# Strassen pairs of w_up: relu and squares behind the next pair's first copy, weight splits beside earlier work

## The chip, the cores and the metric

One NeuronCore of a Trainium2 chip runs the whole program in one launch. The metric is device time in microseconds, the median of several executions. Below, PE is TensorE, ACT ScalarE, DVE VectorE, POOL GpSimd and SP SyncE; POOL and SP only issue DMAs at the places spoken of here.

## The reference

Two transformer layers (`DEPTH = 2`) and then one further layer of another kind, over 1024 tokens of width 1024 in float32. What the change touches is the feed-forward part of the first two layers, of width 4096:

```python
for i in range(DEPTH):
    ...
    hn = rmsnorm(h, norm2[i])
    h = h + jnp.square(jax.nn.relu(hn @ w_up[i])) @ w_down[i]
    ...
```

## The kernel before

Every float32 operand of a matmul is split into a high part, which is float32r, and a low part, the remainder; a product is three matmuls (high by high, high by low, low by high) that add up in one bank of PSUM. A matmul has a stationary 128x128 weight and 512 moving columns. A split of a 128x1024 tile is a copy on ACT (`whi` or `hidh`) and a subtraction on DVE (`wlo` or `hidl`).

`w_up` has 32 output tiles of 128 rows, called units. Units 0 to 7 and 30, 31 are plain (`up`: 8 tiles of the contraction by 3 matmuls by 2 halves of 512 tokens, 48 in all). Units 8 to 29 are computed in pairs by Strassen's scheme, with 7 products instead of 8: 11 pairs in each layer. A product (`prod`, line 1210) is 4 tiles of the contraction by 3 matmuls, 12 in all; a pair is 84. The products come in this order: 1 (A11) into bank P, 2 (S2) into Q, 3 (A12) again into P, 4 (S3) again into Q, 5 (S1) into R, 6 (A22) again into Q, 7 (S4) again into R. Between them ACT and DVE take the banks out: `t1` is ACT's copy of P after product 1 (line 1236), which product 3 must wait for since it adds into the same bank; `u2` and `u3` are DVE's sums of Q and t1; `c1` and `c2` are the two result tiles, to which relu and square are applied on ACT before POOL stores them to DRAM (`keep`, line 1122, tensor `hidd`).

The weights of a pair come as two tiles (`wst`, three buffers, loaded by SP in the order of a plan). `seven` (line 1071) is a generator that splits them, and forms the sums that the scheme wants, into 7 tiles `wsp` out of a ring of 8 buffers, which plain units' `whi` and `wlo` share. Its steps are: A11 and A12 together, A22, four sums on DVE, S2, S3 and S1 together, S4. During a pair the steps of the next pair's weights are called by hand between the products: the first after product 4, two after 5, one after 6, the rest after 7. The weights of the first pair are split in one go behind unit 7.

All engines run their instructions in the order in which the program issues them. Background work is called by `tick`: `spawn` registers a generator that is advanced once for so many microseconds of matmuls, and `advance` splits the weights of plain units up to two ahead, as long as no more than four are held.

After the pairs, units 30 and 31 are plain, and then `w_down` is done in 8 chunks of 4 hid tiles: `fetch` loads the 4 raw tiles of a chunk from `hidd` by POOL, `parts` splits them (`hidh`, `hidl`), and PE adds up products `pd`. The h tiles to which these are added are loaded by POOL behind the first fetch.

Of the kernel before, what the change touches and what calls it, by code (L numbers as in the profile page):

```python
# [2 lines left out]

# [13 lines left out]
AF = mybir.ActivationFunctionType  # L17
# [51 lines left out]
class K:  # L69
# [117 lines left out]
    RAW = ("old", "mg", "w_out2")  # L187

    def is_raw(self, key):
        return key[0] in self.RAW or key[0] == "w_up" and self.SEVEN[0] <= key[2] < self.SEVEN[1]  # L190

    def source(self, key):
        name = key[0]
# [918 lines left out]
    def mlp(self, i, nm, h):  # L1112
# [3 lines left out]
        nc = self.nc  # L1116
        nm.rest(h)
        xs = nm.xs
        box = {}
        lo_, hi_ = self.SEVEN  # L1120

        def keep(m, t):
            nc.gpsimd.dma_start(self.hidd[m], t)

        def up(m, turns=False):
            t = []

            def done(ps, cs):
                if not t:
                    t.append(self.st("hid"))  # L1130
                if "xs" in box:
                    nc.scalar.activation(t[0][:, cs], ps, AF.Relu)
                else:
                    nc.vector.scalar_tensor_tensor(t[0][:, cs], ps, 0.0, box["bc"][:, cs], OP.max, OP.mult)

            self.gemm(("w_up", i, m), xs, done, turns)
            nc.scalar.activation(t[0], t[0], AF.Square)
            keep(m, t[0])

# [21 lines left out]
        def sums():  # L1161
            for p in range(4):
# [13 lines left out]
                b = None  # L1176
                yield

        ta, tb = [], []
        ps = [self.pair("pu") for _ in range(2)]  # L1180
        self.duo([("w_up", i, m) for m in range(2)], xs, ps, cols)
# [4 lines left out]
        for m, pp in enumerate(ps):  # L1186
            t = self.st("hid")
# [4 lines left out]
        t = ps = None  # L1192
        up(3, True)
        xs = nm.xs = None
        box["go"] = True
        self.finish(box["apply"])
        xs = box["xs"] = box.pop("new")
        box["bc"] = None
        sm = self.spawn(sums(), 2.4)
        up(4, True)  # L1200
        for m in range(5, lo_):
            up(m)
            if m == lo_ - 2:
                self.finish(sm)
        A, B = self.HALVES
        view = lambda ts, cs: [(hi[:, cs], lo[:, cs]) for hi, lo in ts]
        x = {"B11": view(xs[0:4], A), "B21": view(xs[4:8], A), "B22": view(xs[4:8], B),
# [2 lines left out]
        def prod(ps, wn, xn, first=False, last=False):  # L1210
            mm = nc.tensor.matmul
            wh, wl = w[wn]
            for k, (xh, xl) in enumerate(x[xn]):
                c = slice(k * 128, (k + 1) * 128)
                mm(ps, wh[:, c], xh, start=first and k == 0, stop=False, skip_group_check=True)  # L1215
                mm(ps, wh[:, c], xl, start=False, stop=False, skip_group_check=True)
                mm(ps, wl[:, c], xh, start=False, stop=k == 3, skip_group_check=True)  # L1217
                if k % 2:
                    self.tick(1.36)
# [1 line left out]
        self.live, self.gone = self.SPLIT_BUFS, []  # L1221
        add = lambda o, p, q: nc.vector.tensor_tensor(o, p, q, OP.add)  # L1222
        pairs = list(range(lo_, hi_, 2))
        gen = self.seven(*[("w_up", i, lo_ + e) for e in range(2)])
        for w in gen:
            pass
        for m in pairs:
            ahead = iter(())
            nxt = None
            if m + 2 < hi_:  # L1230
                ahead = self.seven(*[("w_up", i, m + 2 + e) for e in range(2)])
            P, Q, R = (self.bank("p7") for _ in range(3))
            t1, u2, u3 = (self.k2("u7") for _ in range(3))
            c1, c2 = (self.st("hid") for _ in range(2))
            prod(P, "A11", "B11", True)
            nc.scalar.activation(t1, P, AF.Copy)  # L1236
            prod(Q, "S2", "T2", True)
            add(u2, Q, t1)
            prod(P, "A12", "B21")
            nc.scalar.activation(c1[:, A], P, AF.Relu)  # L1240
            prod(Q, "S3", "T3")
            add(u3, Q, t1)
            nxt = next(ahead, None)
            prod(R, "S1", "T1", True)
            add(c2[:, B], u3, R)
            next(ahead, None)
            next(ahead, None)
            prod(Q, "A22", "T4")
            add(c2[:, A], Q, t1)
            nc.scalar.activation(c2, c2, AF.Relu)  # L1250
            next(ahead, None)
            prod(R, "S4", "B22")
            add(c1[:, B], u2, R)
            nc.scalar.activation(c1[:, B], c1[:, B], AF.Relu)
            for _ in ahead:
                pass
            for n, t in enumerate((c1, c2)):
                nc.scalar.activation(t, t, AF.Square)
                keep(m + n, t)
            t = c1 = c2 = P = Q = R = t1 = u2 = u3 = None  # L1260
            w = nxt
        x = w = ta = tb = nxt = ahead = gen = None
        box.pop("apply")
        self.drop(self.SPLIT_BUFS)

        def fetch(c):
            r = [self.st("hid") for _ in range(4)]
            for q in range(4):
                nc.gpsimd.dma_start(r[q], self.hidd[4 * c + q])
            return r  # L1270

        raw = fetch(0)
        for k in range(8):
            h[k] = self.st("h")
            nc.gpsimd.dma_start(h[k], self.hd[k])
        hid = []

        def parts(n):
            for _ in range(n):
                hid.append(self.split(raw.pop(0), "hid"))  # L1280

        up(30)
        parts(2)
        up(31)
        xs = box["xs"] = None
        parts(2)
        nn = self.norm(self.g[:, i * 24 + 16:i * 24 + 24])
        for c in range(8):
            now, hid = hid, []
# [773 lines left out]
```

## Time and profile before

| what | value |
|---|---|
| median of 3 runs | 3298.48 us (3297.35 to 3300.71) |
| the profiled execution | 3301.77 us, span 3300.0 us |
| busy share of the span: PE, DVE, ACT, POOL | 96%, 59%, 39%, 9% |
| pairs of the first layer | about 513 to 745 us of the span |
| pairs of the second layer | about 1736 to 1969 us of the span |

The page says how long each engine was busy. Who waited for whom is a view of its own, with the total, the count and the longest wait. The order of time lists every instruction with its start, its duration and, in brackets, how long its engine was idle before it and what ended that. A matmul's duration overlaps with the next one's, so the distance of two starts tells the pace.

### The profile page before, as it was taken

How to read it: one execution, taken by the hardware profiler on the slowest of the kernel's cores; microseconds unless marked ns; L12 is line 12 of the kernel's file. 1: busy time of each engine (PE TensorE's matmuls, PEld its weight loads, DVE VectorE, ACT ScalarE, POOL GpSimd, SP SyncE). 2: the span in 40 equal slices, each digit the busy share in tenths (PEclk: the TensorE clock that was granted, in tenths of full speed). 3: DMA queues.
4: the chain of work that ended last, by engine and by line, in shares of the span. 5: the costliest groups of instructions: out<-in, count | busy, mean ns of one | idle time of the engine just before them, and what ended most of it. 6: DMA issues, size and time to landing. Idle time of an engine off the chain costs nothing. (4 is left out here: it accounts for less than half of the span.)

```text
span 3300.0 us, 39088 instructions
## 1 busy us (share of the span) xinstructions
PE 3176.3 (96%) x15332; PEld 2644.0 (80%) x15332; DVE 1961.0 (59%) x3044; ACT 1287.3 (39%) x2128; POOL 312.0 (9%) x479
## 2 busy tenths in 40 slices
PE   8999999999999999999999989999999999999998
PEld 7888787777888888888887777888888787788877
DVE  7666564443444556666564443444655888887465
ACT  4666343333111323666343332111333555554330
POOL 5122000001000002121000011000000000001100
PEclk9999999999999999999999999999999999999999
DMA  4112332335222113222422335222113333335561
GB/s 157 45 51 77 118 112 80 102 102 220 92 96 90 40 50 121 57 58 66 143 87 91 98 107 222 102 97 65 45 39 110 83 95 78 86 90 147 159 211 64
DMA packets 94681, 326.33 MB, mean 99 GB/s; under 512 B 13552, under 2 KB 13728, under 8 KB 94496
## 3 DMA queue, kind: packets, MB, share of 16 engines
q1 hardware_dynamic: 50256, 178.11, 17.0%
q0 software_dynamic: 42944, 141.25, 14.4%
q10 hardware_dynamic: 1296, 4.46, 0.3%
q8 instruction: 121, 1.98, 0.2%
q14 instruction: 64, 0.52, 0.1%
HBM read 244.93 MB, written 75.69 MB: 97 GB/s over the span
## 5 line engine op out<-in xcount | busy, mean ns | idle before, releaser
L311 ACT ACTIVATE whi<-wst 128x1024 fp32r<-128x1024 f32 x214 | 223.4, 1054 | 678.8 <-PE pd L261 498.7
L260 PE MATMUL pd<-hidh,whi 128*128 128x512 f32 x1024 | 400.4, 391 | 2.7 <-ACT hidh L323 2.7
L261 PE MATMUL pd<-hidl,whi 128*128 128x512 f32 x1024 | 400.7, 391 | 1.8 <-DVE hidl L324 1.8
L262 PE MATMUL pd<-hidh,wlo 128*128 128x512 f32 x1024 | 400.1, 391 | 0.0
L1307 DVE TENSOR_TENSOR h<-pd,h 128x512 f32<-128x512 f32 x256 | 175.6, 690 | 332.3 <-PE pd L262 332.3
L316 DVE TENSOR_TENSOR wlo<-wst,whi 128x1024 fp32r<-128x1024 f32 x172 | 207.8, 1223 | 100.7 <-ACT whi L311 100.1
L260 PE MATMUL w_in<-nh,whi 128*128 128x512 f32 x560 | 229.6, 410 | 4.9 <-DVE wl L1600 3.6
L260 PEld LDWEIGHTS pd<-hidh,whi 128*128 128x128 f32 x1024 | 193.0, 188 | 43.5 <-ACT hidh L323 3.6
L261 PEld LDWEIGHTS pd<-hidl,whi 128*128 128x128 f32 x1024 | 193.1, 189 | 43.1 <-DVE hidl L324 3.3
L262 PEld LDWEIGHTS pd<-hidh,wlo 128*128 128x128 f32 x1024 | 193.2, 189 | 40.1
L261 PE MATMUL w_in<-nl,whi 128*128 128x512 f32 x560 | 221.1, 395 | 0.0
L262 PE MATMUL w_in<-nh,wlo 128*128 128x512 f32 x560 | 221.0, 395 | 0.0
L518 PE MATMUL pa<-xh,whi 128*128 128x512 f32 x448 | 181.4, 405 | 0.0
L519 PE MATMUL pa<-xl,whi 128*128 128x512 f32 x448 | 177.0, 395 | 0.0
L520 PE MATMUL pa<-xh,wlo 128*128 128x512 f32 x448 | 177.0, 395 | 0.0
L1541 DVE SCALAR_TENSOR_TENSOR cv<-sg,n,cv 128x1023 f32<-128x1023 f32 (+14 forms) x120 | 151.4, 1262 | 0.6
L1215 PE MATMUL p<-nh,wsp 128*128 128x512 f32 x264 | 106.8, 405 | 34.5 <-ACT u L1236 29.1
L260 PEld LDWEIGHTS w_in<-nh,whi 128*128 128x128 f32 x560 | 106.8, 191 | 24.6 <-DVE wl L1600 4.0
L262 PEld LDWEIGHTS w_in<-nh,wlo 128*128 128x128 f32 x560 | 106.6, 190 | 23.6
L261 PEld LDWEIGHTS w_in<-nl,whi 128*128 128x128 f32 x560 | 107.1, 191 | 18.7 <-issue 0.5
L695 ACT ACTIVATE E<-E,stat 128x256 f32<-128x256 f32 (+1 forms) x192 | 87.7, 458 | 65.2 <-DVE stat L693 65.1
L1222 DVE TENSOR_TENSOR u<-p,u 128x512 f32<-128x512 f32 x44 | 30.4, 691 | 135.8 <-PE p L1217 114.5
(455 smaller groups left out, 7595.9 us busy)
## 6 DMA issues: line engine op xcount, KB each, us to landing
wst<-in_w_up_dram SPq DMA_DIRECT2D x64, 512.0 KB, 4.1
hidd<-hid POOLq DMA_DIRECT2D x64, 512.0 KB, 7.0
wst<-in_w_down_dram SPq DMA_DIRECT2D x64, 512.0 KB, 3.7
hid<-hidd POOLq DMA_DIRECT2D x64, 512.0 KB, 6.1
wst<-in_w_in_dram SPq DMA_DIRECT2D x40, 512.0 KB, 4.3
wst<-in_w_qkv_dram SPq DMA_DIRECT2D x36, 512.0 KB, 4.1
wlo<-in_w_in_dram POOLq DMA_DIRECT2D x35, 512.0 KB, 5.7
wst<-in_w_out_dram SPq DMA_DIRECT2D x24, 512.0 KB, 4.2
```

Source lines behind the costliest of these rows:

```text
L260: mm(ps, wh, xh[:, cs], start=k == 0, stop=False)
L261: mm(ps, wh, xl[:, cs], start=False, stop=False)
L262: mm(ps, wl, xh[:, cs], start=False, stop=k == n - 1)
L311: nc.scalar.activation(h, w, AF.Copy)
L316: nc.vector.tensor_tensor(l, w, h.bitcast(F32), OP.subtract)
L518: mm(out, wh, xh, start=k == 0, stop=False)
L519: mm(out, wh, xl, start=False, stop=False)
L520: mm(out, wl, xh, start=False, stop=k == 7)
L695: nc.scalar.activation(Eh, Eh, AF.Exp, scale=-1.0, bias=stat[:, j, h:h + 1], accum_out=stat[:, j, 4 + h:5 + h])
L1215: mm(ps, wh[:, c], xh, start=first and k == 0, stop=False, skip_group_check=True)
L1307: lambda ps, cs: nc.vector.tensor_tensor(h[m][:, cs], ps, h[m][:, cs], OP.add))
L1541: nc.vector.scalar_tensor_tensor(acc[:, d:1024], C[:, 0:1024 - d], cw[:, j, 30 - d:31 - d], acc[:, d:1024], OP.mult, OP.add)
```

## The change

What a pair does to its result at the end (relu of half of c1, two squares, two stores) becomes a function `post`, which is called in the next pair right behind the copy t1, and behind the last pair once more. The first pair's weights are split by a background generator during unit 7 (the first five steps of `seven`) and the rest behind unit 7. Units 30 and 31 are marked raw, so that `advance` leaves them alone, and are split by hand: 30 behind product 4 of the last pair, 31 behind product 7. The fetch of the first chunk of hid tiles moves from behind the pairs to behind product 5 of the last pair, when the tiles of `ta` are given free; two of the four splits of that chunk stand ahead of unit 30 and two ahead of unit 31, where they stood behind 30 and behind 31.

```diff
--- before.py
+++ after.py
@@ -1,3 +1,4 @@
+import itertools
 import math
 from contextlib import ExitStack
 
@@ -187,7 +188,7 @@
     RAW = ("old", "mg", "w_out2")
 
     def is_raw(self, key):
-        return key[0] in self.RAW or key[0] == "w_up" and self.SEVEN[0] <= key[2] < self.SEVEN[1]
+        return key[0] in self.RAW or key[0] == "w_up" and key[2] >= self.SEVEN[0]
 
     def source(self, key):
         name = key[0]
@@ -1122,7 +1123,7 @@
         def keep(m, t):
             nc.gpsimd.dma_start(self.hidd[m], t)
 
-        def up(m, turns=False):
+        def up(m, turns=False, u=None):
             t = []
 
             def done(ps, cs):
@@ -1133,7 +1134,10 @@
                 else:
                     nc.vector.scalar_tensor_tensor(t[0][:, cs], ps, 0.0, box["bc"][:, cs], OP.max, OP.mult)
 
-            self.gemm(("w_up", i, m), xs, done, turns)
+            if u:
+                self.unit("w_up", self.wk(u), xs, done)
+            else:
+                self.gemm(("w_up", i, m), xs, done, turns)
             nc.scalar.activation(t[0], t[0], AF.Square)
             keep(m, t[0])
 
@@ -1175,6 +1179,12 @@
                 tb.append(self.split(b, "tb"))
                 b = None
                 yield
+
+        def fetch(c):
+            r = [self.st("hid") for _ in range(4)]
+            for q in range(4):
+                nc.gpsimd.dma_start(r[q], self.hidd[4 * c + q])
+            return r
 
         ta, tb = [], []
         ps = [self.pair("pu") for _ in range(2)]
@@ -1198,10 +1208,17 @@
         box["bc"] = None
         sm = self.spawn(sums(), 2.4)
         up(4, True)
+        w = {}
         for m in range(5, lo_):
+            if m == lo_ - 1:
+                ahead = self.seven(*[("w_up", i, lo_ + e) for e in range(2)])
+                gen = self.spawn((w.update(x) for x in itertools.islice(ahead, 5)), 1.5)
             up(m)
             if m == lo_ - 2:
                 self.finish(sm)
+        self.finish(gen)
+        for x in ahead:
+            w.update(x)
         A, B = self.HALVES
         view = lambda ts, cs: [(hi[:, cs], lo[:, cs]) for hi, lo in ts]
         x = {"B11": view(xs[0:4], A), "B21": view(xs[4:8], A), "B22": view(xs[4:8], B),
@@ -1221,9 +1238,7 @@
         self.live, self.gone = self.SPLIT_BUFS, []
         add = lambda o, p, q: nc.vector.tensor_tensor(o, p, q, OP.add)
         pairs = list(range(lo_, hi_, 2))
-        gen = self.seven(*[("w_up", i, lo_ + e) for e in range(2)])
-        for w in gen:
-            pass
+        post, raw, last = None, None, []
         for m in pairs:
             ahead = iter(())
             nxt = None
@@ -1234,6 +1249,8 @@
             c1, c2 = (self.st("hid") for _ in range(2))
             prod(P, "A11", "B11", True)
             nc.scalar.activation(t1, P, AF.Copy)
+            if post:
+                post()
             prod(Q, "S2", "T2", True)
             add(u2, Q, t1)
             prod(P, "A12", "B21")
@@ -1241,8 +1258,13 @@
             prod(Q, "S3", "T3")
             add(u3, Q, t1)
             nxt = next(ahead, None)
+            if m + 2 == hi_:
+                last.append(self.split_w(self.take("w_up", i, hi_)))
             prod(R, "S1", "T1", True)
             add(c2[:, B], u3, R)
+            if m + 2 == hi_:
+                del x["T1"], x["T3"], ta
+                raw = fetch(0)
             next(ahead, None)
             next(ahead, None)
             prod(Q, "A22", "T4")
@@ -1251,25 +1273,24 @@
             next(ahead, None)
             prod(R, "S4", "B22")
             add(c1[:, B], u2, R)
-            nc.scalar.activation(c1[:, B], c1[:, B], AF.Relu)
             for _ in ahead:
                 pass
-            for n, t in enumerate((c1, c2)):
-                nc.scalar.activation(t, t, AF.Square)
-                keep(m + n, t)
-            t = c1 = c2 = P = Q = R = t1 = u2 = u3 = None
+
+            def post(m=m, c1=c1, c2=c2):
+                nc.scalar.activation(c1[:, B], c1[:, B], AF.Relu)
+                for n, t in enumerate((c1, c2)):
+                    nc.scalar.activation(t, t, AF.Square)
+                    keep(m + n, t)
+
+            c1 = c2 = P = Q = R = t1 = u2 = u3 = None
             w = nxt
-        x = w = ta = tb = nxt = ahead = gen = None
+        x = w = tb = nxt = ahead = gen = sm = None
+        last.append(self.split_w(self.take("w_up", i, hi_ + 1)))
+        post()
+        post = None
         box.pop("apply")
         self.drop(self.SPLIT_BUFS)
 
-        def fetch(c):
-            r = [self.st("hid") for _ in range(4)]
-            for q in range(4):
-                nc.gpsimd.dma_start(r[q], self.hidd[4 * c + q])
-            return r
-
-        raw = fetch(0)
         for k in range(8):
             h[k] = self.st("h")
             nc.gpsimd.dma_start(h[k], self.hd[k])
@@ -1279,11 +1300,11 @@
             for _ in range(n):
                 hid.append(self.split(raw.pop(0), "hid"))
 
-        up(30)
         parts(2)
-        up(31)
-        xs = box["xs"] = None
+        up(hi_, u=last[0])
         parts(2)
+        up(hi_ + 1, u=last[1])
+        xs = box["xs"] = last = None
         nn = self.norm(self.g[:, i * 24 + 16:i * 24 + 24])
         for c in range(8):
             now, hid = hid, []
```

ACT at the boundary between the first layer's first two pairs (hid_4644 and hid_4645 are c1 and c2 of the first pair before, hid_4646 and hid_4647 after; hid_4776 and hid_4771 are c1 of the next one; p7 is bank P, wsp a split weight; line numbers behind the change are those of the changed file). Before:

```order
L1250 ACTIVATE hid_4645<-hid_4645 128x1024 [waits DVE_49]
L1090 ACTIVATE wsp_4742<-wst_4490 128x512
L1254 ACTIVATE hid_4644<-hid_4644 128x512 [waits DVE_49]
L1082 ACTIVATE wsp_4759<-wst_4565 128x1024 [waits PE_49,Activation_49]
L1090 ACTIVATE wsp_4763<-wst_4490 128x512 [waits PE_49]
L1258 ACTIVATE hid_4644<-hid_4644 128x1024 [waits Activation_49]
L1258 ACTIVATE hid_4645<-hid_4645 128x1024
L1236 ACTIVATE u7_4773<-p7_4770 128x512 [waits PE_49]
L1240 ACTIVATE hid_4776<-p7_4770 128x512 [waits DMASW1_49,PE_49]
```

After:

```order
L1272 ACTIVATE hid_4647<-hid_4647 128x1024 [waits DVE_49]
L1091 ACTIVATE wsp_4742<-wst_4490 128x512
L1083 ACTIVATE wsp_4758<-wst_4565 128x1024 [waits PE_49]
L1091 ACTIVATE wsp_4762<-wst_4490 128x512 [waits PE_49]
L1251 ACTIVATE u7_4768<-p7_4765 128x512 [waits PE_49]
L1280 ACTIVATE hid_4646<-hid_4646 128x512 [waits DVE_49]
L1282 ACTIVATE hid_4646<-hid_4646 128x1024 [waits Activation_49]
L1282 ACTIVATE hid_4647<-hid_4647 128x1024
L1257 ACTIVATE hid_4771<-p7_4765 128x512 [waits DMASW1_49,PE_49]
```

The copy u7 (t1 of the next pair) moved from behind the relu and the two squares to ahead of them, and the two splits from behind the relu to ahead of it. What the relu of the next c1 waits for (DMASW1) is the same.

ACT at the start of the first layer's pairs (hid_4585 before and hid_4600 after are unit 7's result, wst_4335 and wst_4415 the first pair's weights). Before:

```order
L1132 ACTIVATE hid_4585<-w_up_4558 128x512 [waits PE_49]
L1132 ACTIVATE hid_4585<-w_up_4587 128x512 [waits PE_49]
L1137 ACTIVATE hid_4585<-hid_4585 128x1024 [waits Activation_49]
L1082 ACTIVATE wsp_4617<-wst_4335 128x1024 [waits DMAHW6_49]
L1090 ACTIVATE wsp_4621<-wst_4415 128x512 [waits DMAHW7_49]
L1090 ACTIVATE wsp_4628<-wst_4335 128x512 [waits DVE_49]
L1082 ACTIVATE wsp_4631<-wst_4415 128x1024
L1090 ACTIVATE wsp_4635<-wst_4335 128x512 [waits DVE_49]
L1236 ACTIVATE u7_4641<-p7_4638 128x512 [waits DMASW5_49,PE_49]
```

After:

```order
L1083 ACTIVATE wsp_4575<-wst_4335 128x1024 [waits DMAHW6_49]
L1091 ACTIVATE wsp_4587<-wst_4415 128x512 [waits DMAHW7_49]
L1133 ACTIVATE hid_4600<-w_up_4558 128x512 [waits PE_49]
L1091 ACTIVATE wsp_4609<-wst_4335 128x512 [waits DVE_49]
L1083 ACTIVATE wsp_4618<-wst_4415 128x1024
L1133 ACTIVATE hid_4600<-w_up_4602 128x512 [waits PE_49]
L1141 ACTIVATE hid_4600<-hid_4600 128x1024 [waits Activation_49]
L1091 ACTIVATE wsp_4637<-wst_4335 128x512 [waits DVE_49]
L1251 ACTIVATE u7_4643<-p7_4640 128x512 [waits DMASW5_49,PE_49]
```

Two of the five splits moved from behind unit 7's square to ahead of its first relu, two to between its relus; one stays behind the square.

ACT at the end of the first layer's pairs (whi of wst_5740 and wst_5752 are units 30 and 31, the further whi are w_down's; hid_5946 and hid_5947, after hid_5941 and hid_5942, are the last c1 and c2; hidh is a split of a fetched tile). Before:

```order
L1240 ACTIVATE hid_5946<-p7_5940 128x512 [waits DMASW3_49,PE_49]
L1250 ACTIVATE hid_5947<-hid_5947 128x1024 [waits DMASW4_49,DVE_49]
L1254 ACTIVATE hid_5946<-hid_5946 128x512 [waits DVE_49]
L1258 ACTIVATE hid_5946<-hid_5946 128x1024 [waits Activation_49]
L1258 ACTIVATE hid_5947<-hid_5947 128x1024
L311 ACTIVATE whi_6069<-wst_5740 128x1024 [waits DMAHW4_49]
L311 ACTIVATE whi_6088<-wst_5752 128x1024 [waits DMAHW5_49]
L311 ACTIVATE whi_6092<-wst_5870 128x1024 [waits DMAHW6_49,PE_49]
L311 ACTIVATE whi_6096<-wst_5882 128x1024 [waits DMAHW7_49,PE_49]
L1132 ACTIVATE hid_6112<-w_up_6073 128x512 [waits PE_49]
L1132 ACTIVATE hid_6112<-w_up_6114 128x512 [waits PE_49]
```

After:

```order
L1257 ACTIVATE hid_5941<-p7_5935 128x512 [waits DMASW3_49,PE_49]
L312 ACTIVATE whi_6000<-wst_5740 128x1024 [waits DMAHW4_49]
L1272 ACTIVATE hid_5942<-hid_5942 128x1024 [waits DMASW4_49,DVE_49]
L312 ACTIVATE whi_6054<-wst_5752 128x1024 [waits DMAHW5_49]
L1280 ACTIVATE hid_5941<-hid_5941 128x512 [waits DVE_49]
L1282 ACTIVATE hid_5941<-hid_5941 128x1024 [waits Activation_49]
L1282 ACTIVATE hid_5942<-hid_5942 128x1024
L324 ACTIVATE hidh_6079<-hid_6019 128x1024 [waits DMASW7_49,PE_49]
L324 ACTIVATE hidh_6083<-hid_6020 128x1024 [waits DMASW0_49,PE_49]
L312 ACTIVATE whi_6102<-wst_5870 128x1024 [waits DMAHW6_49]
L312 ACTIVATE whi_6106<-wst_5882 128x1024 [waits DMAHW7_49,PE_49]
L312 ACTIVATE whi_6110<-wst_6010 128x1024 [waits DMAHW0_49,PE_49]
L1133 ACTIVATE hid_6126<-w_up_6087 128x512
```

The splits of units 30 and 31 moved from behind the last squares into the last pair, two splits of fetched tiles came in ahead of w_down's weights, and a third split of w_down's weights stands ahead of unit 30's first relu. On POOL the four fetches of the chunk come ahead of the last two stores instead of behind them.

## Rows read from the trace of the kernel before

**Rows 1.** The page, part 1: busy us, share of the span, instructions.

```profile
PE 3176.3 (96%) x15332; PEld 2644.0 (80%) x15332; DVE 1961.0 (59%) x3044; ACT 1287.3 (39%) x2128; POOL 312.0 (9%) x479
```

**Rows 2.** Waits of PE: who waited for whom, us in total, times, longest.

```profile
PE p L1215 <- ACT u L1236: 29.1, 20, 1.5
...
PE w_up L260 <- ACT whi L311: 8.8, 2, 4.4
```

**Rows 3.** Order of time, PE at a boundary of pairs: start, duration, engine, instruction.

```profile
555.21 0.39 PE L1215 MATMUL p<-nh,wsp 128*128 128x512 f32 x1
...
563.14 0.39 PE L1217 MATMUL p<-tbh,wsp 128*128 128x512 f32 x1
...
565.32 0.39 PE L1216 MATMUL p<-nl,wsp 128*128 128x512 f32 x1
```

**Rows 4.** Order of time, ACT at the same boundary.

```profile
560.46 0.63 ACT L1254 ACTIVATE hid<-hid 128x512 f32<-128x512 f32 x1 [1.36 <-DVE hid L1222]
560.99 1.04 ACT L1082 ACTIVATE wsp<-wst 128x1024 fp32r<-128x1024 f32 x1
...
562.46 1.99 ACT L1258 ACTIVATE hid<-hid 128x1024 f32<-128x1024 f32 x2
564.36 0.57 ACT L1236 ACTIVATE u<-p 128x512 f32<-128x512 f32 x1
```

**Rows 5.** Order of time, PE around the first pair of each layer.

```profile
512.46 0.39 PE L262 MATMUL w_up<-nh,wlo 128*128 128x512 f32 x1
...
520.81 0.39 PE L1215 MATMUL p<-tbh,wsp 128*128 128x512 f32 x1
...
1735.46 0.39 PE L262 MATMUL w_up<-nh,wlo 128*128 128x512 f32 x1
...
1745.97 0.43 PE L1216 MATMUL p<-tbl,wsp 128*128 128x512 f32 x1
```

**Rows 6.** Order of time, DVE at the first pair's first split, first layer.

```profile
515.55 1.22 DVE L1083 TENSOR_TENSOR wsp<-wst,wsp 128x1024 fp32r<-128x1024 f32 x1 [15.04 <-ACT wsp L1082]
```

**Rows 7.** Order of time, PE from the last pair into unit 30, both layers.

```profile
744.89 0.39 PE L1217 MATMUL p<-nh,wsp 128*128 128x512 f32 x1
...
756.22 0.39 PE L262 MATMUL w_up<-nh,wlo 128*128 128x512 f32 x1
...
1969.29 0.39 PE L1217 MATMUL p<-nh,wsp 128*128 128x512 f32 x1
...
1981.49 0.43 PE L261 MATMUL w_up<-nl,whi 128*128 128x512 f32 x1
```

**Rows 8.** Order of time, ACT, DVE and POOL behind the first layer's last pair.

```profile
748.60 2.93 ACT L311 ACTIVATE whi<-wst 128x1024 fp32r<-128x1024 f32 x3
...
749.67 3.50 DVE L316 TENSOR_TENSOR wlo<-wst,whi 128x1024 fp32r<-128x1024 f32 x3 [3.67 <-ACT whi L311]
...
749.51 1.58 POOL L1269 DMA_DIRECT2D hid<-hidd  x3
```

**Rows 9.** Order of time, PE at the first w_down products, both layers.

```profile
775.98 0.39 PE L262 MATMUL pd<-hidh,wlo 128*128 128x512 f32 x1
...
783.61 0.39 PE L260 MATMUL pd<-hidh,whi 128*128 128x512 f32 x1
...
2000.83 0.39 PE L262 MATMUL pd<-hidh,wlo 128*128 128x512 f32 x1
...
2008.95 0.39 PE L262 MATMUL pd<-hidh,wlo 128*128 128x512 f32 x1
```

**Rows 10.** Stretches: window, us, PE busy (matmuls), granted clock, DMA share, GB/s.

```profile
521.00:744.90 223.90, 209.36 (x912) 1.00 0.30 99
744.90:757.00 12.10, 7.64 (x20) 0.72 0.64 221
```

**Rows 11.** The page, part 6: queue, count, KB each, median us to landing.

```profile
hidd<-hid POOLq DMA_DIRECT2D x64, 512.0 KB, 7.0
```

**Rows 12.** DMA issues from 740 to 800 us, the same columns.

```profile
hid<-hidd POOLq DMA_DIRECT2D x12, 512.0 KB, 9.2
```

## Prediction

> **What bounds the kernel now.** The page's busy times come first: TensorE is busy for 96% of the span [rows 1], so the time falls only where TensorE waits or runs at its lower clock. The list of who waited for whom comes second: its longest line on the tensor engine is the matmul of line 1215 waiting for the copy of line 1236, 20 times and 29.1 us, never over 1.5 [rows 2]. Another large one is the unit after the pairs, waiting for its weights [rows 2]. The order of time comes third, because an idle time is less than what a gap costs. In it matmuls start every 0.2266 us: 35 starts from 555.21 to 563.14 [rows 3]. A gap's price is the time between two matmuls less 0.2266 for each start between them. In the 224 us of the first layer's pairs the granted clock is 1.00 and the DMA engines are at 0.30 [rows 10], so those gaps cost no clock. In the 12 us behind the pairs it is 0.72 [rows 10], of levels 1.2 and 2.4 GHz: there the gap brings a stretch at the lower one, and belongs with it to the price.
>
> **What the gaps cost, and what the change does to each.**
>
> *Ten boundaries in each layer.* From 563.14 to 565.32 there are two starts: 2.18 less 0.45 is 1.73 us [rows 3]. ScalarE's rows say why. Product 1 of the next pair (12 matmuls from 557.93, which is 555.21 and 12 steps) ends about 560.8, yet t1 (line 1236) copies it only at 564.36, behind c1's relu, two splits and 1.99 us of squares; it ends at 564.93, and product 3, due at 563.37, adds into the same bank [rows 4]. The change puts relu and squares behind t1. The relu at 560.46 waited 1.36 us for VectorE [rows 4]; the splits behind it need not wait for that, so ScalarE is free from 559.10. The S3/S1 split takes 1.04 [rows 4], S4's half-sized one no more: 561.18. Then t1's 0.57: 561.75 at the latest, 1.6 us before product 3 is due. The relu (0.63) and squares (1.99) then end at 564.4, before the next ScalarE work, which needs product 3's end at 566.1. The queue POOL stores c1 and c2 that much later; nothing in the pairs reads them. VectorE's order in the pairs does not change; what it does after product 4 waits for TensorE itself, so it moves along. Gain: 20 times 1.73, 34.5 us. If the cover were gone, the cost is what t1 is late, as now.
>
> *First pair of each layer.* From the last matmul of unit 7 to the second product's first there are 13 starts in the first layer (512.46 to 520.81): 8.35 less 2.95 is 5.40 us; in the second 17 starts (1735.46 to 1745.97): 10.51 less 3.85 is 6.66 [rows 5]. The change splits these weights during unit 7, 48 matmuls or 10.9 us. VectorE was idle for 15.04 us before its first split of this pair [rows 6]; its eight operations there, at 1.22 for the longest [rows 6], are 9.8 at most. Only S4 stays behind unit 7, and product 7 is the first to need it. The 8 split buffers allow it: unit 7 holds two, the first six tiles take those of units 4 to 6. t1 of this pair stands behind unit 7's square and one split, some 3 us after unit 7, and is due 5.4 after. I take all of it: 12.06 us. The other end is 0.
>
> *Unit 30.* From the last pair's last matmul to full pace again: 15 starts in 11.33 us (744.89 to 756.22), 7.93; in the second layer 17 starts in 12.20 (1969.29 to 1981.49), 8.35 [rows 7]. In the trace ScalarE takes the weights of units 30 and 31 and of the first w_down up only at 748.60, 0.98 us each, and VectorE follows at 749.67, 1.17 each [rows 8]. The change issues both units' splits beside the last pair, which splits nothing for a next pair: 30 after product 4, three products ahead; 31 before the last relu. Nothing of them is left on the path. Gain 16.28; the other end, were the splits late by their own length, is about half.
>
> *First w_down products.* They wait for the split of the stored hid tiles: 13 starts in 7.63 us (775.98 to 783.61) cost 4.68, 15 in 8.12 (2000.83 to 2008.95) cost 4.72 [rows 9]. In the trace two of the four splits stood behind unit 31. Now two stand ahead of unit 30's relu and two ahead of unit 31's. With T for the end of the pairs: squares end at T+3.6, two hid splits at T+5.6, two w_down splits at T+7.6. A third w_down split waits for the buffer that unit 30 holds, until T+10.9, and unit 30's relus, its square and the last two hid splits are queued behind it on ScalarE. At 0.98 for a whole tile and 0.6 for a half they end at T+16.1, VectorE's part at T+17.3. TensorE needs them at T+21.8 (96 starts). Margin 4.5 us; unit 30's banks are not needed before the pairs' banks are used up. Gain 9.40; the other end is 0.
>
> *The loads that move.* POOL issues the four hid loads after product 5 of the last pair, two products or 5.4 us before T, ahead of the last two stores and the eight h loads. At the 9.2 us to landing of the crowded stretch [rows 12] the last lands near T+5.4, 1.6 of it for issuing four, before its split. POOL's three issues from 749.51 took 1.58 us, 0.53 each, while VectorE ran its splits of two SBUF inputs from 749.67 to 753.17 [rows 8]: no delay shows. The Trainium skill (SBUF — State Buffer, section "SBUF: two separate sides") says that GpSimd, which writes the descriptors of DMAs from POOL's queue, can be locked out of SBUF while VectorE holds their shared ports. By that rule the loads, now among VectorE's adds of the last pair, could land late, which is the second rival below; by the row they don't.
>
> **Sum.** 34.5 + 12.06 + 16.28 + 9.40 = 72.3 us. The profiled execution took 3301.77 us, a span of 3300.0 and 1.77 around it: 3229.5 by this sum. It lies 3.29 above the median of the runs, 3298.48, so the forecast for the median is 3226.2.
>
> **Rivals.**
>
> 1. *The boundary stays.* t1 is still behind the S3/S1 and S4 splits, and these wait for buffers that products of the ending pair read. If the last of those products were 7, they would start at 558.3 at the earliest, still before 559.10; and by the rotation of eight buffers over seven tiles it is product 5. For it speaks that next weights come by DMA, which does not move with TensorE: a pair shrinks from 20.8 us (84 steps and 1.73) to 19.0. Against it, DMA is at 0.30 [rows 10]. If all 34.5 stay: 3260.7.
>
> 2. *The w_down start stays.* The hid loads land late, and as they head ScalarE's queue, everything behind them is late. It decides from 4.5 us of lateness in the last two splits. For it: the DMA engines are crowded there, 9.2 us for 512 KB [rows 12]. Then 9.4 stays: 3235.6.
>
> 3. *Slower.* c1 and c2 of a pair are held into the next one. If the tile that the next c1 takes were the one that is just being stored, its first relu (ScalarE, after product 3) would wait for the store. That store is issued after the relu and the first square, about 563.4; the relu is due at 566.5, 3.1 later. At the store's 7.0 us to landing [rows 11] it would be 3.9 late; if nothing hid that, 20 times 3.9 is 78 us, which eats the gain: 3304. It decides from 6.7 us to landing; at 9.2, 122 us and 3348. Against it: 36 tiles rotate, and in the order of the changed kernel the relu waits for a store of two units earlier, some 25 us old.
>
> **How the numbers follow.** All four gone: 0.80, 3226. Rival 2: 0.10, 3236. Rival 1, whole or in part: 0.07, up to 3261. Rival 3: 0.03, of which 0.02 over 0.2% slower and 0.01 within it. About 0.2%, 6.6 us, is what a measurement of this kernel can tell from no change. The range takes in the first two cases: above, 3235.6 and the 2.2 by which the highest run lies over the median, 3238; below, the runs' own spread of 3.4 and half as much again for the lower-clock stretches, which differ by 1.3 between the layers [rows 5], 3221. Faster 0.97, same 0.01, slower 0.02.
>
> **What would show it.** In the changed trace: no wait of the pairs' matmuls for t1; 84 starts in 19.0 us from pair to pair; granted clock 1.00 from unit 7 through the first w_down products; ScalarE's relu and squares right behind t1; unit 30 following the last product at 0.23. Wrong would be a wait under another name at product 2 or 4, at the first w_down product for hid's split or the hid load, or a relu of c1 waiting for a store.

## Result and the profile after

| | before | after |
|---|---|---|
| median of four runs | 3299.01 us | 3225.41 us (3225.20 to 3227.86) |
| ratio | 1 | 0.9779, 95% interval 0.9762 to 0.9796 |
| profiled execution, and its span | 3301.77 us, 3300.0 us | 3227.86 us, 3226.0 us |

The forecast was 3226 us (3226.2 by its sum), in a range from 3221 to 3238. Line numbers below are those of the changed kernel; its matmuls of a pair are lines 1232 to 1234, t1 is line 1251, c1's relu behind product 3 line 1257, the late relu line 1280, the squares line 1282.

Part 1 of the page of after, busy time of each engine, answers [rows 1]: TensorE's busy share rises from 96% to 98%, with the same number of matmuls.

```profile
PE 3152.0 (98%) x15332; PEld 2634.0 (82%) x15332; DVE 1959.4 (61%) x3044; ACT 1289.7 (40%) x2128; POOL 311.7 (10%) x479
```

The top of the list of who waited for whom, on TensorE of after (us in total, times, longest). The two lines of [rows 2], p waiting for t1 and w_up for whi, are gone; what leads the list lies outside the changed stretch and was there before.

```profile
PE pu L336 <- ACT xh L61: 9.5, 2, 9.2
PE S L1599 <- DVE wl L1621: 7.1, 4, 2.4
```

The order of time on TensorE of after (start, duration, engine, instruction), from unit 7's last matmul to the first product with w_down, in both layers:

```profile
512.09 0.39 PE L263 MATMUL w_up<-nh,wlo 128*128 128x512 f32 x1
512.32 0.39 PE L1232 MATMUL p<-nh,wsp 128*128 128x512 f32 x1
...
743.52 0.39 PE L261 MATMUL pd<-hidh,whi 128*128 128x512 f32 x1
...
1700.04 0.39 PE L263 MATMUL w_up<-nh,wlo 128*128 128x512 f32 x1
1700.27 0.39 PE L1232 MATMUL p<-nh,wsp 128*128 128x512 f32 x1
...
1931.47 0.39 PE L261 MATMUL pd<-hidh,whi 128*128 128x512 f32 x1
```

Both stretches take 231.43 us. They hold 1021 starts (eleven pairs of 84, two units of 48, and one), and 1021 times 0.2266 is 231.4: TensorE does not pause once, where it paused at the boundaries of pairs [rows 3], 20 times in all [rows 2], at the first pair [rows 5] and before unit 30 [rows 7]. The windows of after (us, PE busy and its matmuls, granted clock, DMA share, GB/s) show the same, and the clock at its upper level throughout, where [rows 10] had 0.72 behind the pairs:

```profile
512.30:721.50 209.20, 209.20 (x924) 1.00 0.33 118
721.50:733.00 11.50, 11.50 (x52) 1.00 0.84 278
733.00:743.00 10.00, 10.00 (x46) 1.00 1.03 415
743.00:753.00 10.00, 10.00 (x45) 1.00 0.90 323
```

ScalarE of after at the boundary of the first two pairs, which answers [rows 4]:

```profile
531.91 0.61 ACT L1091 ACTIVATE wsp<-wst 128x512 fp32r<-128x512 f32 x1
532.43 1.05 ACT L1083 ACTIVATE wsp<-wst 128x1024 fp32r<-128x1024 f32 x1
533.38 0.61 ACT L1091 ACTIVATE wsp<-wst 128x512 fp32r<-128x512 f32 x1
534.28 0.60 ACT L1251 ACTIVATE u<-p 128x512 f32<-128x512 f32 x1 [0.28 <-PE p L1234]
534.77 0.62 ACT L1280 ACTIVATE hid<-hid 128x512 f32<-128x512 f32 x1
535.42 2.01 ACT L1282 ACTIVATE hid<-hid 128x1024 f32<-128x1024 f32 x2
539.72 0.60 ACT L1257 ACTIVATE hid<-p 128x512 f32<-128x512 f32 x1 [2.28 <-PE p L1234]
```

The three splits run without a break, and t1 now waits 0.28 us for TensorE, where TensorE waited for t1. It ends at 534.88; product 3 starts at 536.80, 1.9 us later. Relu and squares end at 537.4 and leave ScalarE idle for 2.28 us. The next pair's t1 starts at 553.32, 19.04 us after this one.

Where the 74.0 us of span went: the same two stretches took 262.39 us before (512.46 to 774.85) and 264.23 (1735.46 to 1999.69), so 30.96 and 32.80 are gone; the pauses of [rows 9] behind them, 4.68 and 4.72, are gone too. That is 73.2 us. The last 0.8 lies outside these stretches. The ends of the two stretches before, the first products with w_down:

```profile
774.85 0.39 PE L260 MATMUL pd<-hidh,whi 128*128 128x512 f32 x1
...
1999.69 0.39 PE L260 MATMUL pd<-hidh,whi 128*128 128x512 f32 x1
```

### The profile page after: what moved, and what is told of

Its sections match the earlier page's. It is cut to its first block, busy times and chain, and to the rows that moved or that the text cites. A ratio compares the mean times of both kernels' runs of the same rounds, so it can differ in the third digit from the quotient of the medians.

```text
span 3226.0 us, 39074 instructions
## 1 busy us (share of the span) xinstructions
PE 3152.0 (98%) x15332; PEld 2634.0 (82%) x15332; DVE 1959.4 (61%) x3044; ACT 1289.7 (40%) x2128; POOL 311.7 (10%) x479
## 5 line engine op out<-in xcount | busy, mean ns | idle before, releaser
L61 ACT ACTIVATE xh<-h,gains 128x1024 fp32r<-128x1024 f32 x56 | 62.3, 1145 | 119.5 <-DVE h L1033 55.9
```

## Experiments

Four kernels make one part of the change each. The unchanged kernel, run between them, had a median of 3298.54 us over eight runs.

**Relu, squares and stores alone.** The part of the change that defines `post` and calls it behind t1; everything else as before.

```diff
             nc.scalar.activation(t1, P, AF.Copy)
+            if post:
+                post()
```

> Of the change only relu, squares and stores behind the next pair's first copy; first pair, units 30 and 31 and the fetch as before. Theory (each gap has its own price, and the four add up): the 20 boundaries go, 34.5 us, about 3264 at a median of 3298.5; the other gaps keep their 5.4, 6.7, 7.9, 8.4 and twice 4.7 us. Rival (the stall only moves while the other waits are there): under 10 us gained, a wait of about 1 us and more at product 2 or 4 of each pair.

Measured: 3264.13 us (3263.48 to 3264.89), ratio 0.9898 (0.9882 to 0.9915). The gain is 34.4 us, 1.72 per boundary. On TensorE the wait for t1 is gone, and the waits that the other parts remove are all still there:

```profile
PE w_up L261 <- ACT whi L312: 8.8, 2, 4.4
...
PE p L1227 <- ACT wsp L1083: 5.4, 2, 2.7
```

**First pair alone.** The weights of the first pair are split during unit 7.

```diff
+            if m == lo_ - 1:
+                ahead = self.seven(*[("w_up", i, lo_ + e) for e in range(2)])
+                gen = self.spawn((w.update(x) for x in itertools.islice(ahead, 5)), 1.5)
             up(m)
```

> Only the split of the first pair's weights beside unit 7. Theory: 12.1 us gained (3286.4), since the stretch at the lower clock belongs to the gap. Rival (only the waits themselves count, the lower clock comes anyway): 2 x (2.88 + 0.11 + 0.69 + 0.10) = 7.6 us, 3290.9, and the granted clock in the first pair stays under 1.00.

Measured: 3286.88 us (3284.80 to 3289.07), ratio 0.9966 (0.9953 to 0.9979): a gain of 11.7, of 12.06 forecast. Of the waits just shown the one for wsp is gone, the one for whi stays. The interval alone (a gain of 6.9 to 15.5 us) would leave room for the rival's 7.6. The trace does not: from 510 to 530 us and from 1727 to 1747 us TensorE is busy throughout at a granted clock of 1.00, so the stretch at the lower clock went with the wait.

**Units 30 and 31, hid fetch and hid splits alone,** and **the units alone**, with fetch and hid splits as before. The edit for unit 30, which both have:

```diff
             nxt = next(ahead, None)
+            if m + 2 == hi_:
+                last.append(self.split_w(self.take("w_up", i, hi_)))
             prod(R, "S1", "T1", True)
```

> Only the end: weights of units 30 and 31 split ahead, fetch moved, hid splits two and two. Theory: 16.3 + 9.4 = 25.7 us gained (3272.8). Rival (the late squares of the last pair, still ahead of everything, keep the hid splits late): about 16 us, 3282, with the wait at the first w_down products left.

> Only the weights of units 30 and 31 split ahead; fetch and hid splits where they were. Theory: 16.3 us gained (3282.2); the wait at the first w_down products stays, 4.7 us in each layer, because two hid splits stand behind unit 31. Rival (that wait was a follower of the late units and goes with them): 25.7 us, 3272.8, as with the whole end.

Measured: 3272.25 us (3270.65 to 3273.53), ratio 0.9922 (0.9907 to 0.9937), for all of the end; 3282.94 us (3279.86 to 3284.33), ratio 0.9953 (0.9938 to 0.9968), for the units alone. So 15.6 us are the units', and 10.7 us more come with fetch and hid splits; the forecast had 16.28 and 9.40, and the runs of one kernel differ by up to 4.5.

The parts add up: 34.4, 11.7 and 26.3 are 72.4 us, and the whole change gives 73.6 between medians. Within the spread of the runs, none of them lives on a pause that another one leaves.

The other kernels start from the changed one. The unchanged kernel beside them: 3297.80 us for the next four, 3297.06 for the last three.

**Hid splits where they were**, the fetch early as in the change:

```diff
-        parts(2)
         up(hi_, u=last[0])
         parts(2)
         up(hi_ + 1, u=last[1])
         xs = box["xs"] = last = None
+        parts(2)
```

> The changed kernel with the fetch early, but two hid splits behind unit 30 and two behind unit 31, as before. Theory: the wait at the first w_down products comes back whole, 9.4 us, 3234.8, with 4.7 in each layer and a granted clock under 1.00 there. Rival (the early loads are what removed it): 3225.4.

Measured: 3238.04 us (3234.64 to 3238.93), ratio 0.9817 (0.9803 to 0.9832), 12.6 us above after, where 9.4 were expected. The trace shows some 9 of them. TensorE at the first products with w_down in the first layer:

```profile
746.51 0.50 PE L261 MATMUL pd<-hidh,whi 128*128 128x512 f32 x1 [1.36 <-ACT hidh L324]
747.77 0.50 PE L262 MATMUL pd<-hidl,whi 128*128 128x512 f32 x1 [0.76 <-DVE hidl L325]
```

Six starts 0.43 us apart instead of 0.2266 follow soon behind, and the granted clock from 745 to 757 us is 0.86. Counted from start to start, this stretch costs 4.7 us, as in [rows 9], and the one in the second layer 4.3. The profiled execution of this kernel has a span of 3235.4, 9.4 above that of after. The other 3 us lie within the spread of the runs: this kernel's differ by 4.3 us, and the profiled execution of after is the slowest of its four, 2.4 above their median.

**Fetch where it was**, the hid splits as in the change:

```diff
-            if m + 2 == hi_:
-                del x["T1"], x["T3"], ta
-                raw = fetch(0)
...
+        raw = fetch(0)
         for k in range(8):
```

> The changed kernel with the fetch of the first chunk back behind the pairs; the hid splits stay two and two. In the trace of before the four loads, issued 4.4 us after the end T of the pairs, let POOL go on at about T+10, 13, 15.5 and 18. Theory (ScalarE's order sets the hid splits, and their margin is some 4 us): the last split ends near T+22 instead of T+17, the last of the four is needed at T+24, so at most 2 us lost against the changed kernel, 3225 to 3228. Second rival of the prediction (late loads bring the wait at w_down back): 9.4 us, 3235.

Measured: 3226.23 us (3225.35 to 3227.14), ratio 0.9784 (0.9769 to 0.9798): no different from after. The loads did come late. ScalarE of this kernel behind the last pair, whose end T is 721.68 here:

```profile
732.15 1.06 ACT L324 ACTIVATE hidh<-hid 128x1024 fp32r<-128x1024 f32 x1 [6.88 <-DMA hid<-hidd]
734.43 1.06 ACT L324 ACTIVATE hidh<-hid 128x1024 fp32r<-128x1024 f32 x1 [1.22 <-DMA hid<-hidd]
735.40 2.94 ACT L312 ACTIVATE whi<-wst 128x1024 fp32r<-128x1024 f32 x3
...
740.30 1.99 ACT L324 ACTIVATE hidh<-hid 128x1024 fp32r<-128x1024 f32 x2
```

The four fetches took 8.1 us to land (median), ScalarE stood idle for 6.88 us, and the last two hid splits end at 742.3, T+20.6, where after has T+15.9 (its rows stand further below). VectorE's part ends at 743.7, 0.3 us after the first product with w_down has started, and still nothing waits: the tiles are read in turn, three matmuls each (the run before paused at the seventh matmul, for the third tile), so the fourth is due 2 us later than the first. So the early fetch buys 4.7 us of margin and no time. What moved the 9.4 us is the place of the splits in ScalarE's queue.

**How late t1 may be.** Two kernels put work back ahead of t1: the relu alone, and the relu and one of the two squares.

```diff
             add(c1[:, B], u2, R)
+            nc.scalar.activation(c1[:, B], c1[:, B], AF.Relu)
             for _ in ahead:
```

The second kernel has this too, and `post` squares c2 alone:

```diff
             for _ in ahead:
                 pass
+            nc.scalar.activation(c1, c1, AF.Square)
```

> The changed kernel with the relu of c1's second half put back ahead of the copy t1; the two squares stay behind it. By the prediction's account t1 then ends at most 0.63 us later than the 561.75 given for it, plus the wait of that relu for VectorE: 563.0 in the worst case against product 3, due at 563.37. It should cost nothing: 3225 to 3228, and no wait of product 3 for t1. Together with the run that puts one square ahead (0.5 us late, 3241.7) it brackets the point from which lateness is paid. Rival: the chain is later than worked out (the relu's wait for VectorE is 1.4 us, as before the change), t1 ends some 0.3 us too late, 20 times 0.3 is 6 us more: 3232.

> The changed kernel with relu and the first of the two squares ahead of the next pair's first copy t1, the second square behind it. Theory (product 3 waits for the end of t1, microsecond for microsecond): t1 ends 0.95 us earlier than before at 563.98 of before's clock, product 3 is due at 563.37, 0.66 lost and 0.11 of slow restart, 20 times 0.77 is 15.4 us: 3240.8. Rival (any wait costs the whole 1.73): 3260.

Measured: 3226.03 us (3223.58 to 3227.52), ratio 0.9782 (0.9768 to 0.9797), with the relu; 3241.72 us (3241.44 to 3242.81), ratio 0.9832 (0.9815 to 0.9848), with relu and square. ScalarE with the relu ahead, then with relu and square ahead; then the waits of TensorE in the second of them:

```profile
532.52 0.63 ACT L1276 ACTIVATE hid<-hid 128x512 f32<-128x512 f32 x1 [1.36 <-DVE hid L1239]
...
534.52 0.58 ACT L1251 ACTIVATE u<-p 128x512 f32<-128x512 f32 x1
```

```profile
533.21 0.63 ACT L1276 ACTIVATE hid<-hid 128x512 f32<-128x512 f32 x1 [1.36 <-DVE hid L1239]
...
535.22 1.04 ACT L1279 ACTIVATE hid<-hid 128x1024 f32<-128x1024 f32 x1
536.17 0.57 ACT L1251 ACTIVATE u<-p 128x512 f32<-128x512 f32 x1
```

```profile
PE p L1232 <- ACT u L1251: 10.1, 20, 0.5
```

With the relu ahead its 1.36 us of waiting for VectorE is back, as in [rows 4], t1 ends at 535.10 and product 3 starts at 535.43: 0.33 us to spare, and nothing is lost. One square more, and t1 ends at 536.74, 0.61 after product 3 was due (a start after the last matmul of product 2, at 535.90). TensorE's matmul comes 0.66 us late and the next one 0.11 more: a pause of 0.78 in all. Twenty times 0.78 is 15.6, and 3241.72 less 3226.03 is 15.7. So the wait has a sharp edge: free down to the last 0.3 us, and paid in full from there on, at each boundary. No clock is lost in it: there is no run of 0.43-us starts behind such a pause, and the granted clock from 521 to 744 us is 1.00.

**A tile that is still being stored.** The third rival, made real: c1 and c2 are taken after `post` has stored the pair before, and two of the 36 tiles are held back so that the ones just stored come round.

```diff
-            c1, c2 = (self.st("hid") for _ in range(2))
             prod(P, "A11", "B11", True)
             nc.scalar.activation(t1, P, AF.Copy)
             if post:
                 post()
+            post = None
+            c1, c2 = (self.st("hid") for _ in range(2))
```

> The changed kernel with two of the 36 tiles held back during the pairs, and c1 and c2 of a pair taken after the last pair's stores are issued, so that the new c1 takes the tile that is just being stored (third rival of the prediction, made true). The relu of c1 is then about 4 us late at 7.0 us to landing. Prediction's price with nothing to hide it: about 80 us, 3305. Theory (what hides it: the A22 split has 4 us until VectorE takes it, S2's low part is needed 0.5 us into product 2): 0.3 us a boundary or nothing, 3225 to 3233.

Measured: 3226.02 us (3224.56 to 3231.47), ratio 0.9786 (0.9771 to 0.9801). ScalarE of this kernel does wait for the store:

```profile
541.81 0.60 ACT L1261 ACTIVATE hid<-p 128x512 f32<-128x512 f32 x1 [3.92 <-DMA hidd<-hid]
```

In after this relu starts 2.92 us behind product 3's first matmul, which was at 537.25 here: due at 540.17, it is 1.64 us late, and TensorE notices nothing. Over the 20 boundaries the relu is 1.5 to 4.9 us late, 48 us in sum. This execution is the slowest of the four, and its pairs lose 1.3 us, counted from start to start, against 0.1 in after. Two doses more store c1 last, one twice (as below), the other five times:

```diff
-                for n, t in enumerate((c1, c2)):
+                for t in (c1, c2):
                     nc.scalar.activation(t, t, AF.Square)
-                    keep(m + n, t)
+                keep(m + 1, c2)
+                for _ in range(2):
+                    keep(m, c1)
```

> As the run in which c1 takes the tile that is just being stored (its relu was 1.6 us late there and nothing was lost), but c1 is stored last, behind both squares and c2's store, and twice. At 4.9 us to landing the relu of the next c1 should start some 4.6 us late. If the prediction's price was right (each us of lateness is paid 20 times), 3226 + 92 = 3318. By the reading of the two engines' rows, the first thing that the late relu can hold is VectorE's split behind it, then VectorE's add that frees the bank of product 7: 4.5 us of cover. So 3226 to 3236.

> As the run before, with c1 stored five times instead of twice: three more stores of 512 KB, some 2 us each, so the relu is about 11 us late. With a cover of 4.5 us: 20 times 6.5 is 130 us, about 3356, and product 7 (or the next pair's first products) waits for VectorE or for a split. If every us were paid: 3226 + 220 = 3446. If nothing is paid even now, 3226, the store has nothing to do with the pairs' time.

Measured: 3248.03 us (3241.01 to 3257.16), ratio 0.9859 (0.9842 to 0.9876), with two; 3429.64 us (3424.07 to 3434.65), ratio 1.04 (1.0385 to 1.0416), with five. Both lie between what the two readings had, and the waits say why. First VectorE, TensorE and ScalarE with five stores, then VectorE and TensorE with two:

```profile
DVE hid L1239 <- DMA hidd<-hid: 191.4, 17, 13.3
...
PE p L1232 <- DVE hid L1239: 157.8, 18, 10.5
...
ACT hid L1261 <- DMA hidd<-hid: 76.8, 19, 5.4
```

```profile
DVE hid L1239 <- DMA hidd<-hid: 29.9, 17, 3.2
...
PE p L1232 <- DVE hid L1239: 6.1, 6, 1.5
```

I had the wrong first waiter: with c1 stored last it is not the relu but VectorE's first add into c2, behind product 5, that meets the late store (17 times in both), and product 7 waits for that add, since the add empties its bank. Nor do stores of the same tile run side by side: the second waits on POOL until the first has landed, so that with five they are issued some 3.2 us apart, where 2 were expected. In after this add ends 1.83 us before product 7 starts. At the pause shown last in this section it comes 9.7 us later behind product 5 than in after, and product 7 comes 7.9 us late: the cover is 1.8 us, not 4.5. Beyond it every us is paid, and with pauses as long as those with five stores the clock too.

With two stores the pairs of the profiled execution lose 17.2 us, counted from start to start. The six waits with their restarts are 7.8 of these. Another 8.2 are lost at product 2, at 17 boundaries, in pauses of under 0.2 us that the list of waits does not show. There the weight S2 comes late: ScalarE's part of its split stands behind c2's relu, which waits for VectorE's second add into c2, and that add comes late behind the first. ScalarE, VectorE and TensorE at one such boundary:

```profile
571.64 0.61 ACT L1091 ACTIVATE wsp<-wst 128x512 fp32r<-128x512 f32 x1
572.28 0.69 DVE L1092 TENSOR_TENSOR wsp<-wst,wsp 128x512 fp32r<-128x512 f32 x1 [1.65 <-ACT wsp L1091]
572.30 0.50 PE L1232 MATMUL p<-tbh,wsp 128*128 128x512 f32 x1
573.03 0.50 PE L1234 MATMUL p<-tbh,wsp 128*128 128x512 f32 x1
```

Product 2's first matmul starts just behind the end of ScalarE's part (572.25), its third just behind the end of VectorE's (572.97). The other three executions of this kernel took 5 to 16 us more than the profiled one; no trace tells where.

TensorE with five stores, the last matmul ahead of a pause and the first behind it:

```profile
577.52 0.39 PE L1234 MATMUL p<-tbh,wsp 128*128 128x512 f32 x1
585.68 0.79 PE L1232 MATMUL p<-nh,wsp 128*128 128x512 f32 x1 [7.77 <-DVE hid L1239]
```

The starts behind it are 0.43 us apart for some 3 us, the 1.2 GHz level; the granted clock from 545 to 577, which holds another such pause, is 0.79. The pairs of this execution lose 202 us, counted from start to start. Of these 157.8 are the waits; the other 44, or 2.5 per pause, are mostly such stretches.

## Why the prediction was right, step by step

- **What bounds it.** TensorE's pauses did, and nothing took their place. No engine became the bound behind them: VectorE is busy for 61%, ScalarE for 40%.
- **Boundaries: 34.5 forecast, 34.4 measured alone.** The step that carried it was the freeing of the splits from the relu's wait. t1 was to end 1.6 us ahead of product 3; it is 1.9. The kernels with relu and square put back show the two ends of that margin. The first rival, weights that come too late or buffers that are not free, did not occur: a pair takes 19.04 us, and its splits wait for nothing that delays t1.
- **First pair: 12.06 forecast, 11.7 alone.** I took the whole pause; VectorE's splits run under unit 7, as the absence of any pause at 512.32 shows. The size is closer than it had to be: the half-clock stretch in it changes from run to run. In the profiled executions of the units alone and of the whole end, which keep this pause, each layer loses 5.3 to 5.4 us, where the second was read as 6.66.
- **Units: 16.28 forecast, 15.6 alone.** The half-clock stretch behind the pause goes with it, as counted.
- **First products with w_down: 9.40 forecast; between after and the kernel with the old places of the splits, the traces show 9.4 by their spans and 9.0 from start to start.** The times given from T (721.76 in after) held on ScalarE. ScalarE and VectorE of after:

```profile
725.26 1.99 ACT L324 ACTIVATE hidh<-hid 128x1024 fp32r<-128x1024 f32 x2
727.15 1.99 ACT L312 ACTIVATE whi<-wst 128x1024 fp32r<-128x1024 f32 x2
732.61 1.06 ACT L312 ACTIVATE whi<-wst 128x1024 fp32r<-128x1024 f32 x1 [3.46 <-PE w_up L262]
...
735.64 1.99 ACT L324 ACTIVATE hidh<-hid 128x1024 fp32r<-128x1024 f32 x2
```

```profile
738.79 1.23 DVE L325 TENSOR_TENSOR hidl<-hid,hidh 128x1024 fp32r<-128x1024 f32 x1 [0.85 <-PE w_up L262]
```

  The hid splits end at T+5.5 (5.6 forecast), the w_down splits at T+7.4 (7.6), the third begins at T+10.9 as it gets unit 30's buffer, the last hid splits end at T+15.9 (16.1). VectorE's last ends at T+18.3, 1.0 later than given: it waited 0.85 us for a matmul of unit 31, a buffer that I had not counted. The margin was 3.5 us instead of 4.5.
- **The second rival** had the right mechanism and too early an edge. The late fetch delays the last splits by 4.7 us, just past the 4.5 given, and costs nothing: the tiles fall due one after the other, where I had all four due at the first product.
- **The third rival** was priced far too high: its price holds only "if nothing hid that", and nearly all of it was hidden. It did not occur in the change: c1's relu waits for TensorE there, not for a store. Where it was made to occur, the store landed in 4.9 us (median of the 20 in the first layer's pairs) instead of the 7.0 of [rows 11]. The relu was 48 us late in sum over the boundaries; 1.3 us of them were paid in the profiled execution, and nothing shows between the medians. A chain of due times from the relu on, as I had made one for t1, would have shown some us of cover. With enough lateness the rival's sign is right: 1.04.
- **POOL beside VectorE.** By the row, I expected the moved loads not to be held up. In after POOL and VectorE overlap at that place:

```profile
716.35 1.58 POOL L1186 DMA_DIRECT2D hid<-hidd  x3 [2.67 <-DMA hidd<-hid]
```

```profile
716.52 0.69 DVE L1239 TENSOR_TENSOR hid<-u,p 128x512 f32<-128x512 f32 x1 [0.90 <-PE p L1234]
```

  Three issues in 1.58 us, 0.53 each, with VectorE's add in the middle of them, and 0.53 or 0.54 for each store at the boundaries. POOL's wait here is for a store to land, not for VectorE, and the four loads landed in 6.1 us (median), where I had taken 9.2. The Trainium skill (SBUF — State Buffer, section "SBUF: two separate sides") has POOL locked out while a VectorE operation holds their shared ports, and names operations in a 2-port mode, or with two inputs in SBUF (these only against a POOL operation that reads SBUF). My prediction put the adds of the last pair under that rule, but they read one input from PSUM (the bank p), so the overlap with this add does not test it. Behind the pairs VectorE runs splits with both inputs in SBUF while POOL issues the h loads:

```profile
726.34 2.36 DVE L325 TENSOR_TENSOR hidl<-hid,hidh 128x1024 fp32r<-128x1024 f32 x2 [2.55 <-ACT hidh L324]
```

```profile
726.47 3.65 POOL L1296 DMA_DIRECT2D h<-hd  x7
```

  Seven issues in 3.65 us are 0.52 each: no delay shows for these either.
- **The sum**: 72.3 forecast, 74.0 of span. Some 0.8 of the difference lies in the changed stretches (30.96 and 32.80 against 30.63 and 32.31 by the terms), 0.8 elsewhere, which is within what the runs differ by.

## What to carry to other kernels

When an engine in order holds the copy that the next products wait for, list what stands ahead of it and move what nobody waits for behind it; the gain is the pause of each repeat. Work that stays ahead of the copy is free as long as the copy ends in time, here down to 0.33 us, and every us beyond is paid. Price a pause from start to start, so that the restart and the half-clock stretch behind a long one are in it, and price a rival's lateness by the due times of all that it holds up, not by the lateness itself. A load that is moved earlier may buy margin only; try it apart from the move that changes the order of the queue.

## What the hardware showed

- Short pauses of TensorE cost no clock here, even when they come at every boundary: 0.51 us of waiting twenty times in the run with relu and square ahead, and 1.45 us at the boundaries of the run with the units alone, are followed by starts some 0.23 us apart after the first or second, and the granted clock of both runs is 1.00 from 521 to 744 us. Waits of 1.36 and 0.76 us close to each other are followed by six starts 0.43 us apart in the run with the old places of the hid splits, and so is a single one of 7.77 us in the run with five stores.
- How long a 512 KB store takes to land differs between these kernels: 7.0 us (median over the kernel) before [rows 11], 4.5 in after, and 2.9 with five stores, most of which go one at a time. I did not forecast the fall from 7.0 to 4.5, and it cost or gave no time that shows. It comes with the later place of the stores: the median is 4.6 in the run with relu, squares and stores alone, 7.0 in those with the first pair, the whole end or the units alone, and 6.1 and 6.8 where the relu, or relu and square, are put back ahead of t1. Before, the two stores of a pair are issued 0.5 and 1.4 us behind the first load of the next weights (563.80 and 564.74, the load at 563.32); in after it is 1.8 and 2.7 us (536.78 and 537.73, the load at 535.01). That these loads slow the stores fits the times; no run moves the loads alone. These lines are part 6 of the page of after, then of the kernel with five stores (count, KB each, median us):

```profile
hidd<-hid POOLq DMA_DIRECT2D x64, 512.0 KB, 4.5
```

```profile
hidd<-hid POOLq DMA_DIRECT2D x152, 512.0 KB, 2.9
```

  The Trainium skill (DMA: Bandwidth & Descriptors, section "Anatomy of one DMA — SWDGE (gpsimd) path") gives a fixed part and a part by size, from which an estimate for 512 KB is 3.2 us. The stores that go one at a time come near it with 2.9; beside other traffic the traces show more, up to a median of 12.1 us for the h loads behind the last pair of after.
